# A two-layer backbone: R and KK as halves of one tile, joint grams, and another order around the recurrence

## Chip, cores and metric

One core of one Trainium2 chip runs the whole program. The metric is device time in microseconds, the median of the runs shown. Engines: TensorE (PE; its weight loads are listed apart as PEld), VectorE (DVE), ScalarE (ACT), GpSimd (POOL), and SyncE (SP), which issues most DMAs.

## The reference, cut to what matters

Two layers work on 768 tokens (256 context, 512 latent) of 1024 channels. In each layer one projection feeds three branches (a bidirectional RWKV-7 recurrence, a convolution of width 31, attention), which are merged; an MLP follows. The change is in the recurrence. For each head of 64 channels and each direction, a state S of 64 x 64 runs over the tokens:

```python
def step(S, inp):
    r_t, w_t, k_t, v_t, kk_t, a_t = inp
    s_kk = jnp.einsum('bhij,bhj->bhi', S, kk_t)
    S = (S * w_t[:, :, None, :]
         - s_kk[..., None] * (kk_t * a_t)[:, :, None, :]
         + v_t[..., None] * k_t[:, :, None, :])
    return S, jnp.einsum('bhij,bhj->bhi', S, r_t)
```

Before it, kk is normalised per head and decays come from a small two-step projection; after it, a "readout" normalises y per head, adds a bonus (a sum over r, keys and r_k, times v) and multiplies by a gate. In layer 1 the context needs no output: there r and the readout are computed for the 512 latent tokens only (T = 512; `lat` is true).

## The kernel before, in words

Channels lie on partitions, two heads (a "pair", rows 0 to 63 and 64 to 127) per 128 partitions; 8 pairs per layer. The 768 tokens are 12 chunks of 64. In chunked form the recurrence of a pair consists of:

- `rw_kk`, `rw_decay`, `rw_keys`, `rw_rows`, `rw_rrows`: elementwise work on VectorE and ScalarE that makes, per direction d, the tile BK (per chunk the two kinds of keys divided by the decay, 128 columns), KK (kk times the decay, `in_k` and `in_kk` reused) and R (r times the decay, `sg` and `in_r` reused). L803 makes KK, L819 makes R. `rw_bonus` starts with L910, which must read r before L819 overwrites it.
- the grams: `rw_lgram` (L830) multiplies BK of a chunk with KK of the chunk, `rw_rgram` (L847) BK with R; each product has 64 columns. VectorE masks the results into GL (L832) and GB (L850). `rw_rgram` also transposes BK (L857) into GB's other half and copies R into KR (L852).
- `rw_seed` and `rw_solve`: the triangular solve on VectorE (L899, L900), in tile A; `rw_rest`: KK transposed and GL times V (L883), on TensorE.
- in the weave of the next pair: `rw_merge`, `rw_batch` (L963, L974), then `rw_chain`, 12 steps in order of time. A step carries the state (L995, L999, scaled by ScalarE at L1001) and adds to the output y the part from the state (L1011) and the part that needs no state (L1013). `rw_readout` ends the pair one weave later.

All this is small work. The large one, the 128-column jobs of the input projection (`fill`, L412; weights split by L328 on ScalarE and L332 on VectorE), is laid between it. `weave` goes round a list of generators, and each `yield us` calls `pe(us)`, which issues `us * ratio` jobs, and `taps`, which issues taps of the convolution on VectorE (L472). While pair p runs merge, batch, chain, pair p+1 goes from kk to solve in the same weave; `wait` and `note` tie the generators together (`b0`, `b1`: batch of a direction done; `s3`, `s7`, `s11`: chain steps done). The ratio of a weave is the number of jobs over `span`, 84 in both layers. The tile framework's own planner may still exchange neighbouring instructions of an engine's queue by its costs.

PSUM tiles for the small work come from `s.g`, two buffers; a gram takes both, one per head. Tiles named by `rt` share memory by alias: `a1` holds ksq, the spread sums, the decay of direction 0 (`sg`) and, for the readout, ysq and the bonus read back; `a2` and `a3` are the halves of A.

Of the kernel before, what the change touches and what calls it, by code (L numbers as in the profile page):

```python
# [21 lines left out]
CTX = 256  # L22
# [25 lines left out]
SCHED = [dict(open=1.3, early=4, tap0=1, tap2=0, step=1.0, merge=1.2, sums=0, rest=9, ln=9, pad=1, last=1.15, span=84),  # L48
         dict(open=1.2, early=5, tap0=0.8, tap2=0, step=1.0, merge=1.4, sums=0, rest=9, ln=9, pad=1, last=0.85, span=84)]
# [27 lines left out]
class Kern:  # L77
# [580 lines left out]
    def rt(s, tag, shape, bufs=1, alias=None):  # L658
        n = int(np.prod(shape[1:]))
        if alias in s.parts:  # L660
            return s.A[:, s.parts[alias]:s.parts[alias] + n]
# [53 lines left out]
    def rw_kk(s, P, p, I):  # L715
# [3 lines left out]
        sq = s.rt("ksq", [128, TOK], alias="a1")  # L719
# [8 lines left out]
        rn = s.head_spread(rn, 0, "a1")  # L728
# [66 lines left out]
    def rw_rows(s, I, Q, lat):  # L795

        nc = s.nc
        k, kk, o = I['k'], I['kk'], CTX if lat else 0
# [5 lines left out]
        Q['KK'] = (k, kk)  # L804
        yield 0.4
# [5 lines left out]

    def rw_rrows(s, I, Q, lat):

        nc, o = s.nc, CTX if lat else 0
        while 'r' not in I or 'bonus' not in Q:
            yield 0.1
# [3 lines left out]
        Q['R'] = (Q['sg', 0], r)  # L820
        yield 0.3

    def rw_lgram(s, Q, d, c0, n):

        nc = s.nc
        BK, GL, KK = s.big['BK', d], s.big['GL', d], s.c64(Q['KK'][d])
        gp = [s.g([128, n, 64]) for h in range(2)]
        for q in range(n):
            for h in range(2):
                nc.tensor.matmul(gp[h][:, q, :], lhsT=BK[ROWS[h], c0 + q].rearrange("p a b -> p (a b)"), rhs=KK[ROWS[h], c0 + q, :], start=True, stop=True)  # L830
        for h in range(2):
            nc.vector.tensor_tensor(out=GL[:, h, c0:c0 + n], in0=gp[h], in1=s.mask(d, h, 0).unsqueeze(1).to_broadcast([128, n, 64]), op=ALU.mult)  # L832
        yield 0.2 * n

    def rw_rgram(s, Q, part, lat):

        nc = s.nc
        cs = [slice(4 * a, 4 * a + 4) for a in ((0, 0), (1, 2), (2, 1))[part]]
        BK, GB, KR = ([s.big[x, d] for d in range(2)] for x in ('BK', 'GB', 'KR'))
        if part or not lat:  # L840
            R = [s.c64(x) for x in Q['R']]
            gp = [s.g([128, 2, 4, 64]) for h in range(2)]
            for d in range(2):
                for q in range(4):
                    u = cs[d].start + q
                    for h in range(2):
                        nc.tensor.matmul(gp[h][:, d, q, :], lhsT=BK[d][ROWS[h], u].rearrange("p a b -> p (a b)"), rhs=R[d][ROWS[h], u, :], start=True, stop=True)  # L847
            for d in range(2):
                for h in range(2):
                    nc.vector.tensor_tensor(out=GB[d][:, h, cs[d], 1], in0=gp[h][:, d], in1=s.mask(d, h, 1).unsqueeze(1).to_broadcast([128, 4, 64]), op=ALU.mult)  # L850
            for d in range(2):
                nc.scalar.activation(out=KR[d][:, 1, cs[d]], in_=R[d][:, cs[d]], func=AF.Copy)  # L852
            yield 1.4
        for d in range(2):
            bk = s.g([128, 4, 2, 64])
            for q in range(4):
                nc.tensor.transpose(out=bk[:, q].rearrange("p a b -> p (a b)"), in_=BK[d][:, cs[d].start + q].rearrange("p a b -> p (a b)"), identity=s.ident)  # L857
            nc.scalar.activation(out=GB[d][:, :, cs[d], 0, :], in_=bk.rearrange("p c h j -> p h c j"), func=AF.Copy)
            yield 0.45
# [14 lines left out]
    def rw_rest(s, Q, d):  # L874
# [11 lines left out]
        for h in range(2):  # L886
            s.rw_transpose(Q['KK'][d], h, lambda par: KM[ROWS[h], par::2, 0, :])
# [92 lines left out]
    def rw_chain(s, Q, lat, note, free):  # L980
# [5 lines left out]
        for k in range(NCH):  # L986
# [15 lines left out]
            if need_y:  # L1002
                fresh = seg not in yp
                if fresh:
                    yp[seg] = s.py.tile([128, 512], F32, tag="y", name="yp")
                for part in ((1, 0) if k else (0,)):
                    for d in range(2):
                        o = (q[d] - 4 * seg) * 64
                        for h in range(2):
                            if part:  # L1010
                                nc.tensor.matmul(yp[seg][ROWS[h], o:o + 64], lhsT=KR[d][ROWS[h], 1, q[d], :], rhs=S[ROWS[h], d], start=fresh, stop=False)  # L1011
                            else:
                                nc.tensor.matmul(yp[seg][ROWS[h], o:o + 64], lhsT=GB[d][:, h, q[d], 1, :], rhs=UV[d][:, h * 12 + q[d], :], start=fresh, stop=d == 1 and k in (3, NCH - 1))  # L1013
                        fresh = False
# [10 lines left out]
    def rw_readout(s, l, P, p, Q, T, dst):  # L1025
# [9 lines left out]
        sq = t("ysq", [128, TOK], alias="a1")  # L1035
# [3 lines left out]
        bv = t("bv", [128, TOK], alias="a1")  # L1039
# [134 lines left out]
    def rwkv_phase(s, l, P, T):  # L1174
# [3 lines left out]
        with ExitStack() as rc:  # L1178
            s.rp = rc.enter_context(tc.tile_pool(name="rw", bufs=1))
            s.alias, s.parts = {'a1': 768}, {'a2': 0, 'a3': 768}  # L1180

            s.A = s.rp.tile([128, 1536], F32, name="A")
            s.dw = s.conv_taps(l, s.rp)
# [26 lines left out]
            def prep(p, I, Q, wait, *held):  # L1210
# [5 lines left out]
            def sums(p, I, Q, wait, note):  # L1216

                return chain(wait('keys'), s.after(I, 'r', 0, chain(par(s.rw_bonus(P, p, I, Q, T), chain(s.rw_rrows(I, Q, lat), note('rows'))))))
# [11 lines left out]
            def grams(I, Q, wait):  # L1230

                return chain(wait('s3', 'rows'), s.rw_rgram(Q, 0, lat), wait('s7'), s.rw_rgram(Q, 1, lat), wait('s11'), s.rw_rgram(Q, 2, lat),
                             s.rw_values(I), s.rw_rest(Q, 0), s.rw_rest(Q, 1))
# [18 lines left out]
            def stages(p, I, Q, wait, note, *held):  # L1252
                g = prep(p, I, Q, wait, *held)
                return [chain(keyed(g, I, Q, note), solve()), sums(p, I, Q, wait, note), grams(I, Q, wait)]

            def keyed(g, I, Q, note):

                done = False
                for us in g:
                    if not done and 'KK' in Q:  # L1260
                        done = True
                        yield from note('keys')
                    yield us
# [6 lines left out]
            ev, wait, note = events('b0', 'b1', 's3', 's7', 's11')  # L1270
            s.weave(F['open'], *stages(0, I, Q, wait, note))
            old = None
            for p in range(8):
                ev, wait, note = events()
                more = p < 7
                if more:
# [3 lines left out]
                    s.conv_jobs(l, P, p + 1, T, s.ocv)  # L1280
# [227 lines left out]
```

## Time and profile before

| | |
|---|---|
| median of 3 runs | 4574.11 us (4558.41 to 4584.1) |
| profiled execution | 4581.7 us |
| its span, first to last instruction | 4579.9 us |
| instructions | 79160 |
| mean granted TensorE clock | 0.938 |
| TensorE / VectorE / ScalarE busy | 95% / 59% / 40% of the span |
| recurrence of layer 0, about | 60 to 1460 us |
| recurrence of layer 1, about | 2640 to 3820 us |

The span is that of the profiled execution alone; 1.8 us of its own time lie around it. A matmul is recorded with the time until its result has drained, and its neighbours overlap it: what one costs is read from start to start, and a group's "busy" is the union of its instructions. The granted clock is a share of full speed, so 0.5 is the lower of two levels.

### The profile page before, as it was taken

The numbers are of one execution on the slowest core, as the hardware profiler recorded it, in microseconds if no ns is written. First come the engines' busy times: TensorE is split into PE (matmuls) and PEld (weight loads), VectorE is DVE, ScalarE is ACT, GpSimd is POOL, SyncE is SP. The second block draws the span as 40 slices with busy tenths as digits, with TensorE's granted clock in tenths as the row PEclk, the third lists the DMA queues.
The fourth block names the chain that finished last, engine by engine and source line by source line (L and its number), as shares of the span: only waits on it lengthen the run. The fifth ranks groups of instructions, "written<-read, shape, count | busy, mean of one in ns | idle before, by whom it ended". The sixth has DMA issues, their size and how long they took to land. (4 is left out here: it accounts for less than half of the span.)

```text
span 4579.9 us, 79160 instructions
## 1 busy us (share of the span) xinstructions
PE 4346.8 (95%) x32512; PEld 3601.1 (79%) x32512; DVE 2719.8 (59%) x5062; ACT 1838.2 (40%) x3474; POOL 255.3 (6%) x221
## 2 busy tenths in 40 slices
PE   6999999999999989899999899999999999898998
PEld 4988888888887669689999677877777785575886
DVE  3677778877873555342333567777786765464344
ACT  3344444444443443332222444444453434444333
POOL 0000000000001021200000100000000001031001
PEclk9899899999999999999999888999897979999998
DMA  4211111111134225443322221111121124142332
GB/s 164 68 41 51 54 57 50 54 48 63 49 97 149 80 91 161 136 138 113 106 88 63 72 59 50 55 56 44 51 61 49 57 70 139 46 139 72 95 96 79
DMA packets 443601, 367.87 MB, mean 80 GB/s; under 512 B 19662, under 2 KB 391528, under 8 KB 437096
## 3 DMA queue, kind: packets, MB, share of 16 engines
q1 hardware_dynamic: 422504, 283.10, 20.6%
q10 hardware_dynamic: 20736, 79.70, 4.8%
q8 instruction: 257, 4.21, 0.4%
q14 instruction: 104, 0.85, 0.1%
HBM read 301.38 MB, written 53.48 MB: 77 GB/s over the span
## 5 line engine op out<-in xcount | busy, mean ns | idle before, releaser
L332 DVE TENSOR_TENSOR wl<-raw,wh 128x512 fp32r<-128x512 f32 x700 | 504.4, 721 | 743.6 <-ACT wh L328 718.2
L328 ACT ACTIVATE wh<-raw 128x512 fp32r<-128x512 f32 x700 | 441.4, 631 | 1210.8 <-PE mm L412 565.3
L412 PE MATMUL mm<-hh,wh 128*128 128x384 f32 (+1 forms) x2072 | 671.4, 384 | 13.2 <-ACT hh L347 4.0
L412 PE MATMUL mm<-hl,wh 128*128 128x384 f32 (+1 forms) x2072 | 646.0, 371 | 6.1 <-POOL hl L330 6.1
L412 PE MATMUL mm<-hh,wl 128*128 128x384 f32 (+1 forms) x2072 | 648.8, 372 | 0.9 <-DVE wl L332 0.9
L412 PEld LDWEIGHTS mm<-hh,wh 128*128 128x128 f32 x2072 | 377.8, 196 | 66.0 <-issue 11.3
L472 DVE SCALAR_TENSOR_TENSOR cv<-u,dw,cv 128x783 f32<-128x783 f32 (+1 forms) x480 | 426.6, 889 | 3.9
L412 PEld LDWEIGHTS mm<-hl,wh 128*128 128x128 f32 x2072 | 391.8, 195 | 38.2 <-POOL hl L330 8.8
L412 PEld LDWEIGHTS mm<-hh,wl 128*128 128x128 f32 x2072 | 393.5, 196 | 32.2 <-issue 4.4
L412 PE MATMUL mm<-oh,wh 128*128 128x384 f32 (+1 forms) x768 | 253.1, 384 | 10.2 <-DVE acc L1334 5.5
L412 PE MATMUL mm<-ol,wh 128*128 128x384 f32 (+1 forms) x768 | 241.4, 367 | 8.6 <-POOL ol L330 8.6
L389 PE MATMUL mm<-hh,wh 128*128 128x384 f32 (+1 forms) x768 | 238.0, 365 | 6.4 <-ACT hh L347 3.6
L389 PE MATMUL mm<-hl,wh 128*128 128x384 f32 (+1 forms) x768 | 237.1, 363 | 6.4 <-POOL hl L330 5.9
L412 PE MATMUL mm<-oh,wl 128*128 128x384 f32 (+1 forms) x768 | 239.3, 365 | 0.0
L389 PE MATMUL mm<-hh,wl 128*128 128x384 f32 (+1 forms) x768 | 234.8, 360 | 0.0
L389 PE MATMUL mm<-fh,wh 128*128 128x384 f32 (+1 forms) x768 | 230.0, 353 | 0.0
L389 PE MATMUL mm<-fh,wl 128*128 128x384 f32 (+1 forms) x768 | 229.9, 353 | 0.0
L389 PE MATMUL mm<-fl,wh 128*128 128x384 f32 (+1 forms) x768 | 229.4, 352 | 0.0
L1001 ACT ACTIVATE S<-sp,lam 128x64 f32<-128x64 f32 x352 | 92.1, 310 | 226.6 <-PE sp L999 210.4
L412 PEld LDWEIGHTS mm<-oh,wh 128*128 128x128 f32 x768 | 140.2, 190 | 51.6 <-ACT wh L328 13.6
L389 PEld LDWEIGHTS mm<-hh,wh 128*128 128x128 f32 x768 | 141.5, 191 | 37.7 <-ACT wh L328 15.9
L900 DVE TENSOR_TENSOR A<-A,Z 128x30 f32<-128x30 f32 (+14 forms) x480 | 158.9, 331 | 12.9
(311 smaller groups left out, 7566.4 us busy)
## 6 DMA issues: line engine op xcount, KB each, us to landing
raw<-in_w_in_dram SPq DMA_DIRECT2D x316, 256.0 KB
raw<-in_w_ff_dram SPq DMA_DIRECT2D x256, 256.0 KB
wmod<-in_w_mod_dram ACTq DMA_DIRECT2D x48, 1024.0 KB
raw<-in_w_branch_dram SPq DMA_DIRECT2D x96, 256.0 KB
z<-f ACTq DMA_DIRECT2D x40, 384.0 KB
gt<-z SPq DMA_DIRECT2D x24, 384.0 KB
raw<-in_w_out_dram SPq DMA_DIRECT2D x32, 256.0 KB
z<-f ACTq DMA_DIRECT2D x32, 256.0 KB
```

The lines of the kernel that those rows point to most:

```text
L328: s.last_hi = nc.scalar.activation(out=hi, in_=src, func=AF.Copy)
L332: nc.vector.tensor_tensor(out=lo, in0=src, in1=hi.bitcast(F32), op=ALU.subtract)
L389: nc.tensor.matmul(ps[:, b, :t1 - t0], lhsT=w[:, k % 4, :], rhs=a[:, t0:t1], start=k == 0 and f == 0, stop=k == KT - 1 and f == 2)
L412: s.last_mm = nc.tensor.matmul(s.jps[:, b, :t1 - t0], lhsT=w[:, k % 4, :], rhs=a[:, t0:t1], start=k == 0 and f == 0, stop=k == KT - 1 and ...
L472: s.tap_pin(nc.vector.scalar_tensor_tensor(out=hold['c'], in0=u[:, k:k + L], scalar=w(k), in1=hold['c'], op0=ALU.mult, op1=ALU.add))
L900: nc.vector.tensor_tensor(out=X[:, k + 1:, 0:k], in0=X[:, k + 1:, 0:k], in1=tm, op=ALU.add)
L1001: nc.scalar.activation(out=Sn[:, d], in_=sp[:, d], func=AF.Copy, scale=Q['lam', d][:, q[d]:q[d] + 1])
```

## The change

Per direction d there is a new tile `E[d]` of 2 x 768 columns: KK in its first half, R in its second. `in_k`, the decay of direction 0, `in_kk` and `in_r` are now parts of the two tiles, so nothing is copied to get there. `rw_front` multiplies BK of a chunk with both halves at once (128 columns; in layer 1's first four chunks with KK alone), four chunks per call, and masks both results. `rw_turn` (transposes of BK) and `rw_readers` (R into KR, one copy per direction) are what is left of `rw_rgram`. R is made inside `rw_rows`, so before the first gram. The decay's last exponentials move ahead of a yield. In `rw_chain`, all stateless products of a segment (4 or 8 chunks) are issued at the segment's first step, then `y0` or `y1` is noted; the fronts of the next pair wait for `y1`, since they write GB. kk, the readout of the pair before and the decays advance side by side (`par`) instead of one after the other. Before the weave of a pair, 8 to 15 jobs are issued at once; `span` is 78 and 76. The readout's squares and bonus now live in `key`, kk's squares and spread sums in `a2`.

```diff
-SCHED = [dict(open=1.3, ..., last=1.15, span=84),
-         dict(open=1.2, ..., last=0.85, span=84)]
+SCHED = [dict(open=1.3, ..., last=1.15, span=78),
+         dict(open=1.2, ..., last=0.85, span=76)]
...
-        sq = s.rt("ksq", [128, TOK], alias="a1")
+        sq = s.rt("ksq", [128, TOK], alias="a2")
...
-        rn = s.head_spread(rn, 0, "a1")
+        rn = s.head_spread(rn, 0, "a2")
...
     def rw_rows(s, I, Q, lat):
...
-        Q['KK'] = (k, kk)
-        yield 0.4
         for d in range(2):
             Q['lam', d] = s.rt("lam%d" % d, [128, 12], 2)
             e = Q['sg', d]
             nc.scalar.activation(out=e, in_=e, func=AF.Exp, scale=CDEC)
             nc.gpsimd.tensor_copy(Q['lam', d], s.c64(e)[:, :, 63 * (1 - d)])
-
-    def rw_rrows(s, I, Q, lat):
-
-        nc, o = s.nc, CTX if lat else 0
-        while 'r' not in I or 'bonus' not in Q:
+        yield 0.4
+        while 'bonus' not in Q:
             yield 0.1
         r = I['r']
         for d, to in ((0, Q['sg', 0]), (1, r)):
             nc.vector.tensor_tensor(out=to[:, o:], in0=r[:, o:], in1=Q['sg', d][:, o:], op=ALU.mult)
-        Q['R'] = (Q['sg', 0], r)
-        yield 0.3
+        yield 0.2
+
+    def rw_front(s, d, g, lat):
+
+        nc = s.nc
+        c = slice(4 * g, 4 * g + 4)
+        n = 1 if lat and g == 0 else 2
+        BK, GL, GB = (s.big[x, d] for x in ('BK', 'GL', 'GB'))
+        E = s.E[d].rearrange("p (x c t) -> p x c t", x=2, t=64)
+        gp = [s.g([128, 4, 2, 64]) for h in range(2)]
+        for q in range(4):
             for h in range(2):
-                nc.tensor.matmul(gp[h][:, q, :], lhsT=BK[ROWS[h], c0 + q].rearrange("p a b -> p (a b)"), rhs=KK[ROWS[h], c0 + q, :], start=True, stop=True)
...
+                nc.tensor.matmul(gp[h][:, q, 0:n, :], lhsT=BK[ROWS[h], 4 * g + q].rearrange("p a b -> p (a b)"),
+                                 rhs=E[ROWS[h], 0:n, 4 * g + q, :], start=True, stop=True)
+        for x, G in ((0, GL[:, :, c]), (1, GB[:, :, c, 1]))[:n]:
+            for h in range(2):
+                nc.vector.tensor_tensor(out=G[:, h], in0=gp[h][:, :, x, :],
+                                        in1=s.mask(d, h, x).unsqueeze(1).to_broadcast([128, 4, 64]), op=ALU.mult)
+        yield 1.0
...
+    def rw_readers(s, lat):
+
+        o = 4 if lat else 0
         for d in range(2):
+            s.nc.scalar.activation(out=s.big['KR', d][:, 1, o:], in_=s.c64(s.E[d][:, TOK:])[:, o:], func=AF.Copy)
+        yield 0.2
...
             if need_y:
-                fresh = seg not in yp
-                if fresh:
+                off = lambda c: (c - 4 * seg) * 64
+                if seg not in yp:
                     yp[seg] = s.py.tile([128, 512], F32, tag="y", name="yp")
-                for part in ((1, 0) if k else (0,)):
+                    for c in (range(4, NCH) if seg else range(4)):
+                        for d in range(2):
+                            for h in range(2):
+                                nc.tensor.matmul(yp[seg][ROWS[h], off(c):off(c) + 64], lhsT=GB[d][:, h, c, 1, :], rhs=UV[d][:, h * 12 + c, :], start=c == 4 * seg and d == 0, stop=False)
+                    note("y%d" % seg)
+                if k:
...
-        sq = t("ysq", [128, TOK], alias="a1")
+        sq = t("ysq", [128, TOK], alias="key")
...
-        bv = t("bv", [128, TOK], alias="a1")
+        bv = t("bv", [128, TOK], alias="key")
...
-            s.alias, s.parts = {'a1': 768}, {'a2': 0, 'a3': 768}
+
+            s.E = [s.rp.tile([128, 2 * TOK], F32, name=f"E{d}") for d in range(2)]
...
+            s.key = s.rp.tile([128, TOK], F32, name="key")
+            s.alias, s.parts = {}, {'in_k': (s.E[0], 0), 'a1': (s.E[0], TOK), 'in_kk': (s.E[1], 0), 'in_r': (s.E[1], TOK),
+                                    'a2': (s.A, 0), 'a3': (s.A, 768), 'key': (s.key, 0)}
...
-                return chain(s.after(I, 'k', 0, s.rw_kk(P, p, I)), *held, s.rw_decay(P, p, Q), wait('b0'), s.rw_keys(P, p, I, Q, 0), wait('b1'), s.rw_keys(P, p, I, Q, 1),
-                             s.rw_rows(I, Q, lat), *(s.rw_lgram(Q, d, c, n) for d in (1, 0) for c, n in ((0, 8), (8, 4))), wait('rows'),
+                return chain(par(s.after(I, 'k', 0, s.rw_kk(P, p, I)), chain(*held), s.rw_decay(P, p, Q)),
+                             wait('b0'), s.rw_keys(P, p, I, Q, 0), wait('b1'), s.rw_keys(P, p, I, Q, 1), note('keys'),
+                             s.rw_rows(I, Q, lat), wait('y1'), *(s.rw_front(d, g, lat) for d in (1, 0) for g in (1, 2, 0)),
                              s.rw_seed(1, slice(0, 12)), s.rw_seed(0, slice(0, 12)))
...
+                return chain(wait('keys', 's3'), s.rw_turn(0, 0), s.rw_turn(1, 0), wait('s7'), s.rw_turn(0, 1), s.rw_turn(1, 2), wait('s11', 'rows'), s.rw_turn(0, 2), s.rw_turn(1, 1),
+                             s.rw_readers(lat), s.rw_values(I), s.rw_rest(0), s.rw_rest(1))
...
                     s.conv_jobs(l, P, p + 1, T, s.ocv)
+                    s.fill(8 + len(s.jobs) % 8)
```

## Rows read from the trace of the kernel before

**Rows 1.** The page, busy us, share of the span and instructions per engine.

```profile
PE 4346.8 (95%) x32512; PEld 3601.1 (79%) x32512; DVE 2719.8 (59%) x5062; ACT 1838.2 (40%) x3474; POOL 255.3 (6%) x221
```

**Rows 2.** Windows, both recurrences: length, busy us (instructions) per engine, granted clock, DMA.

```profile
60.00:1460.00 1400.00, 1371.40 (x13029) 1197.83 (x13030) 1021.16 (x1915) 604.31 (x1209) 22.37 (x40) 0.94 0.20 62
2640.00:3820.00 1180.00, 1130.07 (x10565) 911.22 (x10564) 847.24 (x1730) 533.97 (x1092) 13.11 (x34) 0.89 0.20 60
```

**Rows 3.** Groups by line on PE: out<-in, shapes, count | busy us, mean ns.

```profile
L830 PE MATMUL g<-in_k,BK 64*128 64x64 f32 x768 | 121.2, 348 | 0.0
...
L847 PE MATMUL g<-sg,BK 64*128 64x64 f32 x640 | 95.0, 332 | 0.0
...
L847 PE MATMUL g<-in_r,BK 64*128 64x64 f32 x640 | 88.2, 329 | 0.0
...
L830 PE MATMUL g<-in_kk,BK 64*128 64x64 f32 x768 | 83.0, 323 | 32.4 <-DVE in_kk L803 31.3 <-DVE GL L832 1.1
...
L1013 PE MATMUL yp<-UV,GB 128*64 128x64 f32 x1280 | 76.5, 237 | 0.0
```

**Rows 4.** Timeline of PE, grams of layer 0: start us, us, instruction, count.

```profile
637.90 2.00 PE L830 MATMUL g<-in_kk,BK 64*128 64x64 f32 x32
639.84 0.44 PE L412 MATMUL mm<-hl,wh 128*128 128x384 f32 x1
...
641.08 1.10 PE L830 MATMUL g<-in_kk,BK 64*128 64x64 f32 x8
642.11 0.44 PE L412 MATMUL mm<-hl,wh 128*128 128x384 f32 x1
```

**Rows 5.** Timeline of PE, runs with 64-column weights, layer 0.

```profile
683.64 1.02 PE L883 MATMUL g<-UV,GL 64*64 64x64 f32 x26
684.59 0.44 PE L412 MATMUL mm<-hh,wl 128*128 128x384 f32 x1
...
716.04 1.96 PE L963 MATMUL g<-BK,GL 64*64 64x128 f32 x32
717.94 0.61 PE L412 MATMUL mm<-hh,wh 128*128 128x384 f32 x2
```

**Rows 6.** Windows of 2 us around the grams of that pair, layer 0.

```profile
646.00:648.00 2.00, 2.00 (x26) 2.00 (x25) 1.63 (x4) 0.00 (x0) 0.00 (x0) 1.00 0.00 0
...
656.00:658.00 2.00, 2.00 (x14) 1.88 (x14) 0.94 (x3) 0.00 (x0) 0.00 (x0) 0.50 0.00 0
...
674.00:676.00 2.00, 2.00 (x19) 1.75 (x17) 1.79 (x7) 0.46 (x1) 0.00 (x0) 1.00 0.74 237
```

**Rows 7.** Timeline of PE, first grams of a pair of layer 1.

```profile
3081.91 3.68 PE L830 MATMUL g<-in_kk,BK 64*128 64x64 f32 x32 [7.30 <-DVE in_kk L803]
3085.52 0.79 PE L412 MATMUL mm<-hh,wl 128*128 128x512 f32 x1
```

**Rows 8.** Waits of PE, layer 0, then layer 1: us, times, longest.

```profile
PE g L830 <- DVE in_kk L803: 2.2, 1, 2.2
...
PE g L830 <- DVE in_kk L803: 29.1, 7, 7.3
```

**Rows 9.** Timeline of DVE ahead of that wait, idle time in brackets.

```profile
3055.03 0.75 DVE L1056 SCALAR_TENSOR_TENSOR y<-y,V,bv 128x512 f32<-128x512 f32 x1 [3.12 <-ACT y L1054]
...
3061.13 1.76 DVE L765 TENSOR_TENSOR_SCAN sg<-smask,sg 128x768 f32<-128x768 uint8 x1 [4.09 <-ACT sg L763]
...
3080.90 0.95 DVE L803 TENSOR_TENSOR in_kk<-in_kk,Z 128x768 f32<-128x768 f32 x1
...
3082.98 0.68 DVE L819 TENSOR_TENSOR in_r<-in_r,A 128x512 f32<-128x512 f32 x1
```

**Rows 10.** Groups by line and shape on DVE: the masks.

```profile
L832 DVE TENSOR_TENSOR GL<-g,masks 128x512 f32<-128x512 f32 x64 | 42.5, 688 | 48.6 <-PE g L830 48.4
L832 DVE TENSOR_TENSOR GL<-g,masks 128x256 f32<-128x256 f32 x64 | 26.9, 424 | 79.1 <-PE g L830 78.6
```

**Rows 11.** Window of 20 us behind the wait of layer 1's pair.

```profile
3098.00:3118.00 20.00, 20.00 (x100) 17.59 (x99) 8.25 (x20) 6.33 (x11) 0.00 (x0) 0.57 0.16 48
```

More of the change, by code (lines that the diff above doesn't have):

```diff
@@ L44 @@
 VOFF = {n: 8 * i for i, n in enumerate(VECS)}
-SCHED = [dict(open=1.3, early=4, tap0=1, tap2=0, step=1.0, merge=1.2, sums=0, rest=9, ln=9, pad=1, last=1.15, span=84),
-         dict(open=1.2, early=5, tap0=0.8, tap2=0, step=1.0, merge=1.4, sums=0, rest=9, ln=9, pad=1, last=0.85, span=84)]
+SCHED = [dict(open=1.3, early=4, tap0=1, tap2=0, step=1.0, merge=1.2, sums=0, rest=9, ln=9, pad=1, last=1.15, span=78),
+         dict(open=1.2, early=5, tap0=0.8, tap2=0, step=1.0, merge=1.4, sums=0, rest=9, ln=9, pad=1, last=0.85, span=76)]
 def shape_constants():
@@ L835, in rw_rgram @@
[L835 to L853, printed above, removed]
-        for d in range(2):
[L855 to L859, printed above, removed]
@@ new lines, in rw_front, with rw_turn @@
+        for x, G in ((0, GL[:, :, c]), (1, GB[:, :, c, 1]))[:n]:
[3 more added lines that the diff above has]
+        yield 1.0
+    def rw_turn(s, d, g):
+        nc, c = s.nc, slice(4 * g, 4 * g + 4)
+        BK, GB = (s.big[x, d] for x in ('BK', 'GB'))
+        bk = s.g([128, 4, 2, 64])
+        for q in range(4):
+            nc.tensor.transpose(out=bk[:, q].rearrange("p a b -> p (a b)"), in_=BK[:, 4 * g + q].rearrange("p a b -> p (a b)"), identity=s.ident)
+        nc.scalar.activation(out=GB[:, :, c, 0, :], in_=bk.rearrange("p c h j -> p h c j"), func=AF.Copy)
+        yield 0.45
@@ L1002, in rw_chain @@
             if need_y:
[L1003 to L1004 removed]
+                off = lambda c: (c - 4 * seg) * 64
+                if seg not in yp:
                     yp[seg] = s.py.tile([128, 512], F32, tag="y", name="yp")
[L1006 removed]
+                    for c in (range(4, NCH) if seg else range(4)):
[4 more added lines that the diff above has]
+                if k:
                     for d in range(2):
[L1008 removed]
                         for h in range(2):
[L1010 to L1014, printed above, removed]
+                            nc.tensor.matmul(yp[seg][ROWS[h], off(q[d]):off(q[d]) + 64], lhsT=KR[d][ROWS[h], 1, q[d], :], rhs=S[ROWS[h], d], start=False, stop=d == 1 and k in (3, NCH - 1))
             S = Sn
@@ L1209, in chain, with prep @@
                     yield from g
-            def prep(p, I, Q, wait, *held):
-                return chain(s.after(I, 'k', 0, s.rw_kk(P, p, I)), *held, s.rw_decay(P, p, Q), wait('b0'), s.rw_keys(P, p, I, Q, 0), wait('b1'), s.rw_keys(P, p, I, Q, 1),
-                             s.rw_rows(I, Q, lat), *(s.rw_lgram(Q, d, c, n) for d in (1, 0) for c, n in ((0, 8), (8, 4))), wait('rows'),
+            def prep(p, I, Q, wait, note, *held):
+                return chain(par(s.after(I, 'k', 0, s.rw_kk(P, p, I)), chain(*held), s.rw_decay(P, p, Q)),
+                             wait('b0'), s.rw_keys(P, p, I, Q, 0), wait('b1'), s.rw_keys(P, p, I, Q, 1), note('keys'),
+                             s.rw_rows(I, Q, lat), wait('y1'), *(s.rw_front(d, g, lat) for d in (1, 0) for g in (1, 2, 0)),
                              s.rw_seed(1, slice(0, 12)), s.rw_seed(0, slice(0, 12)))
-            def sums(p, I, Q, wait, note):
-                return chain(wait('keys'), s.after(I, 'r', 0, chain(par(s.rw_bonus(P, p, I, Q, T), chain(s.rw_rrows(I, Q, lat), note('rows'))))))
             def par(*gs):
@@ L1228, in par, with rests @@
                             yield us
-            def grams(I, Q, wait):
-                return chain(wait('s3', 'rows'), s.rw_rgram(Q, 0, lat), wait('s7'), s.rw_rgram(Q, 1, lat), wait('s11'), s.rw_rgram(Q, 2, lat),
-                             s.rw_values(I), s.rw_rest(Q, 0), s.rw_rest(Q, 1))
+            def rests(I, wait):
+                return chain(wait('keys', 's3'), s.rw_turn(0, 0), s.rw_turn(1, 0), wait('s7'), s.rw_turn(0, 1), s.rw_turn(1, 2), wait('s11', 'rows'), s.rw_turn(0, 2), s.rw_turn(1, 1),
+                             s.rw_readers(lat), s.rw_values(I), s.rw_rest(0), s.rw_rest(1))
             def events(*ns):
@@ L1252, in stages @@
             def stages(p, I, Q, wait, note, *held):
[L1253 to L1263, printed above, removed]
+                return [chain(prep(p, I, Q, wait, note, *held), note('rows'), solve()),
+                        chain(wait('keys'), s.after(I, 'r', 0, s.rw_bonus(P, p, I, Q, T))), rests(I, wait)]
             todo_c = lambda p: round((32 - F['rest']) * p / 7)
```

22 lines of the change are left out of this document (8 added, 14 removed).

## The prediction, made before the result was known

> **What bounds the kernel now.** I read the busy shares first: TensorE is busy for 95% of the span, VectorE for 59%, ScalarE for 40% [rows 1]. Then the windows of the two stretches that the change touches, the recurrence of layer 0 and of layer 1: TensorE is busy 1371 of 1400 us and 1130 of 1180 us, VectorE 1021 and 847 us [rows 2]. So TensorE's instruction stream sets the time there, with 28.6 and 49.9 us of gaps; VectorE has about a quarter to spare on average. The same rows give a mean granted clock of 0.94 and 0.89. With two levels, full and half, that is half clock (1.2 GHz) for 12% of 1400 and 22% of 1180, 168 + 260 = 428 us, and costs half of it, 214 us.
>
> Next the costliest instructions of the part that changes. The grams are L830 (with KK) and L847 (with R): 121.2 + 83.0 + 95.0 + 88.2 = 387 us busy for 2 x 768 + 2 x 640 = 2816 instructions, 137 ns each [rows 3]. The code asks for 24 products per direction and pair, 384 in 16 pairs, where the trace counts 768: each fp32 product is two instructions. All are 64 columns against 128-column weights on half of the rows.
>
> The order in time gives their price at full clock, start to start: 32 in 1.94 us, 61 ns each, where the two heads (the two halves of the rows) alternate; 8 in 1.03 us, 129 ns, in a run that I read as one head's, since four chunks give eight instructions per head [rows 4]. In layer 1 the same 32 take 3.61 us after a gap of 7.30 us [rows 7], 113 ns each, at half clock. The clock also falls without a gap: at 646 it is 1.00, at 656 it is 0.50 with TensorE recorded busy for the whole 2 us, at 674 it is back [rows 6]. What ran there was almost only grams.
>
> Last, who is waited for: the first gram waits for VectorE's `in_kk` (L803) once in layer 0 (2.2 us) and 7 times in layer 1, 29.1 us [rows 8]. Before that wait VectorE itself stood still for 3.12 and 4.09 us, behind the readout's copies (L1054) and then behind the decay's ScalarE step (L763) [rows 9]: readout and decay run one after the other.
>
> **The change, part by part.**
>
> (a) Both grams of a chunk in one product of 128 columns. 1280 R instructions and as many of KK become 1280; the 256 of KK left over (layer 1's first four chunks, which need no output: 1536 - 1280) stay. What the 64 further columns cost isn't in the trace for these weights. Nearest rows: with 64-column weights, 26 instructions of 64 columns take 0.95 us (37 ns) and 32 of 128 columns 1.90 us (59 ns), so 64 columns more cost 23 ns where halves alternate [rows 5]; in a one-head run nothing alternates and I take twice that, 46. So a chunk's pair goes from 2 x 61 = 122 to 61 + 23 = 84 ns, and from 258 to 129 + 46 = 175: 31 to 32% less; I use 30. The pairs cost now 183 us (L847) plus 1280/1536 of L830's 204, 170 us: 353 us. 0.30 x 353 = **106 us gained**. Bounds: 0, if the columns alone set the price, and 177 (half of 353), if the weights alone do. I take 106, because both kinds of row show a part that goes with the weights and one that goes with the columns.
>
> (b) Readout, kk and decays side by side, and 8 to 15 jobs issued ahead of each pair's weave, so that k is there when it begins. VectorE's two gaps, 7.2 us together, are as long as the wait of 7.30 us that follows [rows 7, 9]; filling them removes it. Of the 31.3 us of these waits [rows 8] I take **20 gained**; bounds 0 and 31. The jobs ahead are moved, not added: TensorE runs them anyway.
>
> (c) The first gram now needs R too, so it waits for r's product (L819) and not for `in_kk`. In the pair shown `in_kk` begins at 3080.90 and is done 0.95 later, r's product begins at 3082.98 and takes 0.68: 1.8 us later [rows 9]. Queued behind it on TensorE is everything, ordinary jobs included. What covers it is the projection work that the order puts there; without cover 16 x 1.8 = 29 us. I take **15 lost**; bounds 0 and 29.
>
> (d) Stateless outputs of a segment together. The same 1280 instructions, now in runs of 32 and 64 instead of eights; 76.5 us busy, 60 ns each [rows 3]. The long run of 64 columns in [rows 5] went at 37 ns at full clock, so at most (60 - 37) x 1280 = 29 us, and at least nothing, since a part of the 60 is half clock; I stay near the lower end, since the runs that grow are no shorter in columns. **5 gained**.
>
> (e) Masks on VectorE: in a pair of layer 0, 4 of 512 elements and 16 of 256 become 24 of 256: 4 x 0.69 + 16 x 0.42 = 9.5 us against 10.1 [rows 10], 0.6 us more per pair. It hides in VectorE's spare quarter; if not, 10 us in all. Six copies of R on ScalarE become two large ones, on an engine 40% busy: nothing. The squares and spread sums move into the solve's tile A, so they wait for the solve's last transposes; the merge at the same place waits for those already, so nothing. No DMA is added; the bonus reload and g2 are issued earlier on SP's queue, ahead of weights that have slack: nothing.
>
> (f) Clock. Fewer gram instructions in a row, with jobs between, and no gap ahead of them: some of the 214 us comes back. The gram's own part is in (a) already; the jobs that run inside the half-clock stretches are not. **20 gained**, about a tenth; bounds 0 and 107, half.
>
> Sum: 106 + 20 - 15 + 5 + 20 = **136 us gained**. The profiled execution took 4581.7 us; that gives 4446. The median of the runs shown is 4574.1, 7.6 lower, so a median should come out at 4438: I predict **4440**, 3% less.
>
> **Rivals.**
>
> *Weights alone set a gram's price.* Then (a) is 177: 4581.7 - 207 - 7.6 = 4367, and with half of the clock back 4280. For it: 61 ns against 37 for the same columns with half the weights [rows 4, 5]. Against: 23 ns more for the columns in the same rows. Chance 0.2.
>
> *Nothing saved in the grams.* If loads are hidden behind the other head's columns, two products of 64 columns equal one of 128. (a) is 0, and the rest leaves 30 us: 4544; with the waits as they are, 4574. For it: L830 is recorded as busy without a break. Against: the 61 to 37 ns above. Chance 0.11. The Trainium skill, "TensorE: Matmul & The Clock Gate", section "Part 2: What happens when you issue a matmul", speaks for this rival: it says the engine pulls a weight load ahead of running matmuls when their row groups don't conflict, which is just the case of two heads. By that rule the sum would be 30 us instead of 136. This trace agrees only in part: alternating heads do cost 61 ns instead of 129, but the width of the weights still shows.
>
> *Slower: the gate before the first gram.* Now three VectorE products more than before stand between keys and grams in one chain (L803, then the bonus's, then L819). If the order puts no jobs there, every pair stands still as layer 1's do, 7.3 us, and half clock follows: I price that at the 7.3 us and at 0.43 x 20 = 8.6 us lost to the clock in a window of 20 us behind such a wait, granted 0.57 [rows 11]: 16 us per pair, 16 x 16 = 256, against the 151 us of the other terms: 4574 + 105 = 4679. It decides from 151/16 = 9.4 us per pair. For it: seven of layer 1's eight pairs wait there now [rows 8]. Against: layer 0 waits once only, and (b) fills the gaps from which the wait comes. Chance 0.09.
>
> **The numbers.** My forecast has 0.6; its own range is 4390 to 4510, from (a) at 60 to 150 us. Over all cases the range is 4350 to 4560: it takes in the weights-alone case and the nothing-saved case, and leaves out the slower one and the best of the clock. About 0.5% (23 us) is what a measurement of this kernel can tell from no change. Faster by more than that: 0.6 + 0.2 + 0.03 = 0.83; within: 0.08; slower: 0.09.
>
> **What would show it.** Gram instructions: 1536 instead of 2816, with about 85 ns each where heads alternate and busy time near 280 us in place of 387. The wait of the first gram on VectorE, now for r's product, under 31 us in all. Mean granted clock in the recurrences at or above 0.94 and 0.89. Windows of both recurrences about 8 us per pair shorter, TensorE still over 96% busy. I'm wrong if grams keep 115 ns or more per instruction at full clock, or if TensorE's gaps in the recurrences grow by over 60 us.

## The result and the profile after

The changed kernel takes 4303.18 us (median; 4295.91 to 4305.05) against 4574.11 us of the kernel before: ratio 0.9409, 95% interval 0.9373 to 0.9444, so 271 us or 5.9% less. A fourth run of the kernel before took 5619.48 us, far from its other three, and is left out of both figures. The result is faster, as predicted, but 137 us below the forecast of 4440 and 47 us below the range. The profiled execution took 4305.05 us, with a span of 4303.3 us.

The page after, busy us and share of the span per engine, answers to [rows 1]:

```profile
PE 4083.1 (95%) x31232; PEld 3360.6 (78%) x31232; DVE 2712.4 (63%) x5126; ACT 1829.2 (43%) x3426; POOL 254.8 (6%) x221
```

TensorE is busy 263.7 us less with 1280 instructions fewer, and its gaps (span less busy) go from 233.1 to 220.2 us. The two make the 276.6 us by which the span is shorter. VectorE and ScalarE have as much to do as before.

The windows of the recurrences after (length, busy us per engine, granted clock) answer to [rows 2]; layer 1 now begins earlier:

```profile
60.00:1460.00 1400.00, 1366.53 (x12805) 1165.87 (x12806) 1090.74 (x2088) 665.24 (x1312) 39.47 (x49) 0.98 0.23 72
2480.00:3680.00 1200.00, 1146.11 (x10657) 887.49 (x10656) 929.63 (x1943) 604.85 (x1223) 23.75 (x42) 0.96 0.23 71
```

TensorE is the bound as before; its granted clock rose from 0.94 and 0.89 to 0.98 and 0.96, and over the whole span from 0.938 to 0.969. With two levels that is 2 x (1 - 0.938) x 4579.9 = 568 us at half clock before and 267 us after: 301 us less, worth 150 us. After, the recurrences end some 170 us before these windows do, before some 40. From a layer's first product into y to its last, it took 1152 us before and 1032 after in layer 0, and 1016 and 897 in layer 1: 119 us less in each, 15 us per pair.

The gram and stateless groups after (busy us, mean ns | idle before, its releasers) answer to [rows 3]; L828 is the joint gram, L1001 the stateless output:

```profile
L828 PE MATMUL g<-E,BK 64*128 64x128 f32 x1280 | 125.7, 285 | 12.6 <-ACT key L912 6.9 <-DVE GB L832 3.3 <-DVE E L815 2.1
L1001 PE MATMUL yp<-UV,GB 128*64 128x64 f32 x1280 | 54.9, 226 | 0.0
L828 PE MATMUL g<-E,BK 64*128 64x64 f32 x256 | 20.3, 277 | 0.3 <-DVE GB L832 0.2
```

The four groups of [rows 3] can't simply be added up for a comparison: the two with R (95.0 and 88.2 us) run in between each other and overlap. Busy time of their line, L847, in the kernel before, with the overlap counted once (length, PE, its loads, clock, DMA):

```profile
0.00:4580.00 4580.00, 150.46 (x1280) 143.68 (x1280) 0.94 0.26 80
```

With L830's 204.15 us, and 2 us in which the two lines overlap, grams cost 352.5 us before for 2816 instructions, 125 ns each, and not the 387 us that the prediction went by. After, they cost 146.0 us for 1536, 95 ns each. So 206 us went: 1280 x 125 = 160 by the count, and 1536 x (125 - 95) = 46 because each of the others is cheaper too. What made those cheaper is the clock. By the starts and the granted clock in the two traces, 1096 of the 2816 instructions began at half clock, on average 176 ns ahead of the next start, and the other 1720 took 88 ns; after, none of the 1536 began at half clock, and they took 90 ns. At full clock, 1280 instructions fewer are worth 1280 x 88 = 113 us. With 150 us of clock and 13 us of gaps that makes the 276 us of the span.

The lines also show the waits ahead of the grams: 12.9 us in all, 2.1 of them on r's product (L815), where [rows 8] had 31.3 us.

Around them, the jobs of the projection (L412 with `hh` and `hl`), 6216 instructions before and after, fell from 1962.5 to 1903.3 us; the transposes from 70.6 to 56.8; the stateless outputs from 76.5 to 54.9. (Groups overlap at their edges and the rest grew by 13 us, so these sum to more than 263.7.)

TensorE's timeline after, layer 0 (start us, us, instruction, count), gives the price start to start, as [rows 4] did:

```profile
300.91 1.16 PE L828 MATMUL g<-E,BK 64*128 64x128 f32 x16
302.00 0.33 PE L1006 MATMUL yp<-S,KR 64*64 64x64 f32 x2
...
310.68 1.16 PE L828 MATMUL g<-E,BK 64*128 64x128 f32 x8
311.76 0.44 PE L412 MATMUL mm<-hh,wh 128*128 128x384 f32 x1
```

16 joint instructions in 1.09 us, 68 ns each; 8 in 1.08 us, 135 ns each. With half of the columns it was 61 (in a run of 32) and 129. I had put 23 and 46 ns on the 64 further columns; they cost 7 and 6 at most, and nothing between runs of one length (split and double, below).

### The profile page after: what moved, and what is told of

It reads as the page before. It is cut to its first block, busy times and chain, and to the rows that moved or that the text cites. A ratio compares the mean times of both kernels' runs of the same rounds, so it can differ in the third digit from the quotient of the medians.

```text
span 4303.3 us, 76623 instructions
## 1 busy us (share of the span) xinstructions
PE 4083.1 (95%) x31232; PEld 3360.6 (78%) x31232; DVE 2712.4 (63%) x5126; ACT 1829.2 (43%) x3426; POOL 254.8 (6%) x221
## 4 chain that ended last, share of the span: by engine, by line
PE 78%; DVE 11%; ACT 4%; issue 3%; DMA 2%; POOL 2%; SPq 0%; ACTq 0%; DVEq 0%; POOLq 0%
PE mm L412 29%; PE mm L389 21%; PE g L828 3%; PE g L634 2%; PE g L955 2%; PE g L966 2%; PE sp L987 2%; PE sp L991 2%; PE S L613 1%; PE g L875 1%; PE g L1071 1%; PE yp L1006 1%; DVE wl L332 1%; DVE A L892 1%; DVE Z L891 1%
## 5 line engine op out<-in xcount | busy, mean ns | idle before, releaser
L412 PE MATMUL mm<-hh,wh 128*128 128x384 f32 (+1 forms) x2072 | 658.9, 378 | 10.0 <-ACT hh L347 4.0
L412 PE MATMUL mm<-hl,wh 128*128 128x384 f32 (+1 forms) x2072 | 626.0, 362 | 7.2 <-POOL hl L330 7.2
L412 PE MATMUL mm<-hh,wl 128*128 128x384 f32 (+1 forms) x2072 | 619.1, 361 | 2.5 <-DVE wl L332 2.4
L412 PEld LDWEIGHTS mm<-hh,wh 128*128 128x128 f32 x2072 | 367.8, 191 | 61.8 <-issue 9.8
L412 PEld LDWEIGHTS mm<-hl,wh 128*128 128x128 f32 x2072 | 383.9, 191 | 34.4 <-POOL hl L330 10.0
L412 PEld LDWEIGHTS mm<-hh,wl 128*128 128x128 f32 x2072 | 384.0, 192 | 29.8 <-DVE wl L332 4.5
L412 PE MATMUL mm<-oh,wh 128*128 128x384 f32 (+1 forms) x768 | 252.3, 383 | 10.4 <-DVE acc L1320 6.0
L412 PE MATMUL mm<-ol,wh 128*128 128x384 f32 (+1 forms) x768 | 240.0, 365 | 10.6 <-POOL ol L330 10.6
L389 PE MATMUL mm<-hh,wh 128*128 128x384 f32 (+1 forms) x768 | 239.1, 366 | 6.3 <-ACT hh L347 3.6
L389 PE MATMUL mm<-hl,wh 128*128 128x384 f32 (+1 forms) x768 | 238.2, 365 | 5.5 <-POOL hl L330 5.0
L412 PE MATMUL mm<-oh,wl 128*128 128x384 f32 (+1 forms) x768 | 239.4, 365 | 0.0
L389 PE MATMUL mm<-hh,wl 128*128 128x384 f32 (+1 forms) x768 | 235.8, 362 | 0.0
L412 PEld LDWEIGHTS mm<-oh,wh 128*128 128x128 f32 x768 | 139.9, 190 | 51.5 <-ACT wh L328 13.6
L389 PEld LDWEIGHTS mm<-hh,wh 128*128 128x128 f32 x768 | 142.2, 192 | 37.7 <-ACT wh L328 15.9
```

Source lines behind the costliest of these rows:

```text
L389: nc.tensor.matmul(ps[:, b, :t1 - t0], lhsT=w[:, k % 4, :], rhs=a[:, t0:t1], start=k == 0 and f == 0, stop=k == KT - 1 and f == 2)
L412: s.last_mm = nc.tensor.matmul(s.jps[:, b, :t1 - t0], lhsT=w[:, k % 4, :], rhs=a[:, t0:t1], start=k == 0 and f == 0, stop=k == KT - 1 and ...
```

## The experiments

Two theories. **Count and price:** a gram costs its weight load, so half as many loads is the gain. **Runs of one half:** where the planner lets one half of the rows stand alone for eight instructions, each costs twice as much and the clock falls with them; the change gains because it has fewer of these. The rival to both is the order of the work around the grams. All runs, with grams as instructions x columns, their mean busy ns each (overlaps counted once), and the mean granted clock of the span:

| run | grams | ns | clock | us, median | ratio to before |
|---|---|---|---|---|---|
| before | 2816 x 64 | 125 | 0.938 | 4572 to 4577 | 1 |
| changed kernel | 1280 x 128, 256 x 64 | 95 | 0.969 | 4303.18 | 0.9409 [0.9373, 0.9444] |
| split | 2816 x 64 | 101 | 0.951 | 4473.95 | 0.9779 [0.9744, 0.9813] |
| double | 2560 x 128, 512 x 64 | 77 | 0.964 | 4421.13 | 0.9681 [0.9637, 0.9725] |
| onehead | as changed | 119 | 0.967 | 4323.21 | 0.9463 [0.9409, 0.9517] |
| serial | as changed | 106 | 0.967 | 4328.98 | 0.9461 [0.9425, 0.9498] |
| noprefill | as changed | 101 | 0.970 | 4325.59 | 0.9454 [0.9421, 0.9487] |
| joint_old_order | as changed | 107 | 0.965 | 4348.11 | 0.9520 [0.9477, 0.9564] |
| split_old_order | 2816 x 64 | 107 | 0.944 | 4490.33 | 0.9827 [0.9765, 0.9889] |
| before_y | as before | 123 | 0.942 | 4567.35 | 1.0007 [0.9978, 1.0037] |
| before_late | as before | 130 | 0.930 | 4606.25 | 1.0078 [1.0041, 1.0115] |
| before_pin | as before | 84 | 0.964 | 4438.99 | 0.9713 [0.9669, 0.9757] |
| before_late_pin | as before | 81 | 0.962 | 4469.98 | 0.9766 [0.9715, 0.9818] |
| pinned | as changed | 93 | 0.966 | 4352.39 | 0.9514 [0.9480, 0.9549] |
| split_pin | 2816 x 64 | 78 | 0.966 | 4428.31 | 0.9678 [0.9619, 0.9738] |
| before_four | as before | 105 | 0.949 | 4545.05 | 0.9936 [0.9911, 0.9961] |
| before_late_four | as before | 135 | 0.922 | 4694.7 | 1.0237 [1.0157, 1.0316] |

**split, double: loads or columns.** Both start from the changed kernel. split issues each joint product as two of 64 columns; double issues it twice at 128.

```diff
+            for x in range(n):                                          # split
                 for h in range(2):
-                    nc.tensor.matmul(gp[h][:, q, 0:n, :], ... rhs=E[ROWS[h], 0:n, 4 * g + q, :], ...)
+                    nc.tensor.matmul(gp[h][:, q, x, :], ... rhs=E[ROWS[h], x, 4 * g + q, :], ...)
+            for twice in range(2):                                      # double: the loop over h, twice
```

> The changed kernel, but each joint product of 128 columns issued again as two products of 64 columns with the same weights: 2816 gram instructions instead of 1536, all else (order, jobs ahead, stateless outputs together) as changed. Theory A, the joint products did it, by their number and through the clock: the gain over the kernel before mostly goes, 4303 + about 87 (1280 more at 68 ns) + most of the clock's part, so 4450 to 4580, with the granted clock of the recurrences back near 0.95 and 0.90. Theory B, the new order gave the clock back and the joint products only saved instructions: 4303 + 80 to 100 = about 4390, granted clock still 0.98 or more.

> The changed kernel with every joint product issued twice (the second overwrites the first with the same values), so 3072 gram instructions of 128 columns: as many weight loads as with split products (2816), with twice the columns. If the number of weight loads sets both price and clock: 4303 + 171 x 1536/1280 = about 4508, half clock around the grams as with split products. If the columns per load decide about the clock: 4303 + 1536 x 68 to 75 ns = 4410 to 4420, granted clock as in the changed kernel (0.98 and 0.96).

The timeline of split, then that of double, for one run of 32 each:

```profile
324.23 2.06 PE L829 MATMUL g<-E,BK 64*128 64x64 f32 x32
326.22 0.63 PE L412 MATMUL mm<-hh,wl 128*128 128x384 f32 x2
```

```profile
302.21 2.06 PE L829 MATMUL g<-E,BK 64*128 64x128 f32 x32
304.19 0.33 PE L1007 MATMUL yp<-S,KR 64*64 64x64 f32 x2
```

32 of 64 columns in 1.99 us and 32 of 128 columns in 1.98: 62 ns each, so in these runs the further columns cost nothing. By that price the 1280 instructions of split are worth 79 us, but split lost 171. The rest goes with the clock: 0.951 is 438 us at half clock, against 267 in the changed kernel, and half of the difference is 86 us; 79 + 86 = 165. In double, with about as many loads (3072 against 2816) and twice the columns, the clock is 0.964, 318 us at half: 1536 x 62 = 95 us and 26 of clock make 121, and it lost 118. The jobs show the clock too: 1940.1 us in split against 1904.8 in double and 1903.3 in the changed kernel.

**onehead: the halves one after the other.** The changed kernel with the two loops exchanged.

```diff
-        for q in range(4):
-            for h in range(2):
+        for h in range(2):
+            for q in range(4):
```

> The changed kernel with the joint products of a call in the other order: four chunks of one head, then four of the other. From the timeline, 68 ns per instruction where heads alternate and 136 where one head runs alone. If that is so, the grams' 146 us busy go to about 1536 x 136 = 209, and the time to 4303 + 60 = 4365, or a little more if the clock falls. If the order of heads doesn't matter: 4303 within 10 us.

```profile
L828 PE MATMUL g<-E,BK 64*128 64x128 f32 x1280 | 150.7, 289 | 6.7 <-DVE E L815 2.2 <-ACT key L912 2.1 <-ACT KR L850 1.2
L828 PE MATMUL g<-E,BK 64*128 64x64 f32 x256 | 34.5, 293 | 0.0
```

These gram groups are 183.0 us together (overlaps counted once), 37 more than before the exchange, and the time grew by 20, not by the 60 expected: many of the changed kernel's groups ran one half alone already (the eights in its timeline). As I read it, the planner exchanges neighbours by when the two PSUM tiles come free; no run shows that. The clock stayed at 0.967 (0.969 in the changed kernel), though more of the joint grams ran as one half alone.

**serial, noprefill, joint_old_order, split_old_order: the order.** serial puts kk, readout and decay one after the other again; noprefill drops the jobs issued ahead; joint_old_order does both and sets `span` to 84, split_old_order adds split.

```diff
-                return chain(par(s.after(I, 'k', 0, s.rw_kk(P, p, I)), chain(*held), s.rw_decay(P, p, Q)),
+                return chain(s.after(I, 'k', 0, s.rw_kk(P, p, I)), *held, s.rw_decay(P, p, Q),
...
-                    s.fill(8 + len(s.jobs) % 8)
```

> The changed kernel with kk, the readout and the decays one after the other again; joint products kept. Theory A (joint products): 4303 to 4330, clock as in the changed kernel. Theory B (the order gave the clock back): 4380 or more, granted clock in layer 1's recurrence under 0.95, waits of the first gram on VectorE back at about 30 us.

> The changed kernel without the 8 to 15 jobs issued ahead of each pair's weave. Theory A: 4303 to 4330. Theory B: 4350 or more, with the first products of the merge waiting for the solve (now 7.7 us in all) and lower granted clock at the start of the pairs.

> The changed kernel with the joint products kept, and the order taken back: kk, readout and decays one after the other, no jobs issued ahead of the weave, span 84 again. If the small effects of these (25 and 22 us, each alone) simply add, 4350; a theory in which one of them covers for the other says 4400 or more, and waits of the first gram on VectorE of 20 us or more as in the kernel before.

> As the kernel joint_old_order, with each joint product split in two products of 64 columns. What stays of the change is the grouping (grams of KK and R of four chunks together, after R is made) and the stateless outputs. Theory A, the splitting costs the same whatever the order: joint_old_order + 171, about 4520. Theory B, the grouping is worth nothing and the rest of the distance was order: within 15 us of the kernel before, 4560 to 4585.

serial loses 26 us, noprefill 22, both together 45: they add. In joint_old_order TensorE is busy for 4085.7 us, as with the new order (4083.1), but its span is 4349.6, so its gaps are 263.9 us and not 220.2. The order's gain is 44 us of gaps. Most of it is one wait of joint_old_order (us, times, longest):

```profile
PE g L909 <- DVE key L902: 40.7, 8, 9.8
```

L909 is TensorE's product in `rw_bonus`, which waits for VectorE's first product there; in the changed kernel it waits 1.7 us. Joint products are worth 4490 - 4348 = 142 us in the old order and 171 in the new one.

**before_y: the stateless outputs alone.** The kernel before with the change's loop over a segment's stateless products in place of its own, and nothing else.

> The kernel before with one part of the change alone: the stateless outputs of a segment issued together at its first step. Both theories: a small gain, 5 to 30 us, 4545 to 4570, from 76.5 us busy for these products down to 50 to 70; half clock around the grams as in the kernel before.

```profile
L1009 PE MATMUL yp<-UV,GB 128*64 128x64 f32 x1280 | 48.0, 229 | 0.0
```

These products take 48.0 us in place of 76.5, and the time is the same. Where those 28 us went isn't shown: the profile is of an execution of 4553.33 us, 14 less than the median.

**before_late, before_four, before_late_four: 87 us not accounted for.** split_old_order has the gram instructions of the kernel before and takes 87 us less. Two parts of the difference were tried on the kernel before, alone and together: the gate ahead of the KK grams, and groups of four chunks. The edit shown is both.

```diff
-                             s.rw_rows(I, Q, lat), *(s.rw_lgram(Q, d, c, n) for d in (1, 0) for c, n in ((0, 8), (8, 4))), wait('rows'),
+                             s.rw_rows(I, Q, lat), wait('rows'), *(s.rw_lgram(Q, d, c, n) for d in (1, 0) for c, n in ((0, 4), (4, 4), (8, 4))),
```

> The kernel before with its KK grams issued only after R is made (as the change does it, but separate products of 64 columns in the old groups). If the distance between the kernel before (4577) and split_old_order (4490) comes from the first gram, which no longer waits for VectorE (31 us) and no longer drops the clock behind such a wait: 4510 to 4545, wait on L803 under 5 us. If it comes from how the two heads follow each other in the grams: within 15 us of 4577.

> The kernel before with the KK grams in three groups of four chunks per direction in place of eight and four; nothing else. Theory A (groups of four release their two PSUM tiles sooner and are what split_old_order has over the kernel before): 40 to 87 us faster, 4490 to 4535, fewer gram us (under 370 of 387 before). Theory B (smaller groups only give the planner more places to put one half alone): no change or slower, 4575 to 4600, gram busy time at 387 us or more.

> The kernel before with both: KK grams in groups of four, and the wait for the readout's rows ahead of them (before_late alone: 4606). Theory A: well under before_late, 4510 to 4560. Theory B: at or above before_late, 4600 or more; then the 87 us of split_old_order come from KK and R of a chunk standing next to each other, and not from the size of a group or the place of the gate.

The later gate alone costs 32 us. The wait on L803 is gone, but TensorE now waits 37.5 us for the bonus's product instead (L917 on L910), and the clock fell to 0.930. Groups of four alone gain 27 us. Both times lie outside of both ranges expected.

```profile
L830 PE MATMUL g<-in_kk,BK 64*128 64x64 f32 x768 | 93.5, 339 | 62.3 <-DVE in_kk L803 62.2
```

There the waits of the first gram doubled, from 31.3 to 62.2 us, and yet the kernel is faster, since the grams fell from 352.5 to 295.1 us. Both together lose 123 us. TensorE's gaps grew from 233.1 to 283.0 us there, and its longest wait is again for the bonus:

```profile
PE g L917 <- DVE key L910: 73.7, 9, 14.2
```

The clock fell too, to 0.922. A window of before_late_four (length, busy us per engine, granted clock):

```profile
816.00:862.00 46.00, 46.00 (x217) 41.40 (x217) 17.87 (x42) 6.54 (x11) 0.00 (x0) 0.52 0.09 26
```

TensorE is recorded busy for all of 46 us, with no gap, at a clock of 0.52. So neither gate nor group size by itself accounts for the 87 us. The grams hold 52 us of it (352.5 before, 300.6 in split_old_order), but before_four's 295.1 are no dearer, and it is still 55 us slower than split_old_order. It waits more: 62.2 us for L803, where split_old_order waits 33.4 us for the bonus. What is left (among other things KK and R of a chunk next to each other, the transposes apart from the grams, two copies of R in place of six) wasn't isolated.

**before_pin, before_late_pin, pinned, split_pin: the order of the halves.** `tap_pin` is the kernel's own helper that keeps an instruction in the order in which the code writes it. Put around the gram products alone, it makes the halves alternate.

```diff
-                nc.tensor.matmul(gp[h][:, q, :], lhsT=BK[...]..., rhs=KK[ROWS[h], c0 + q, :], start=True, stop=True)
+                s.tap_pin(nc.tensor.matmul(gp[h][:, q, :], lhsT=BK[...]..., rhs=KK[ROWS[h], c0 + q, :], start=True, stop=True))
```

> The kernel before with the gram instructions kept in the order of the program on TensorE, so that the two heads alternate throughout (61 ns instead of 129 where one head ran alone). If the one-head runs made the grams dear: gram busy from 387 to under 320 us, time 4577 - 60 to 90 = 4490 to 4520. If the wait of the first gram is the cause: within 15 us of 4577.

> Both of these edits. If the two causes share the 87 us to split_old_order, this kernel comes to 4490 within 20 us; if the grouping by four chunks with R counts by itself, it stays above 4520.

> The changed kernel with its joint products kept in the order of the program, so that heads alternate throughout: 62 to 68 ns instead of 136 where one head ran alone. The grams' 146 us busy go to about 1536 x 68 = 104; if TensorE's stream sets the time, 4303 - 30 to 42 = 4261 to 4273. Rival: a product that must not be overtaken makes the others wait for the masks of the call before (two PSUM tiles only), and the time stays within 10 us of 4303 or rises.

> The changed kernel with each joint product as two products of 64 columns, and these written into TensorE's order so that the two row halves alternate. Compare with pinned (4352, the same with joint products) and split (4474, no pin). Theory (alternating runs cost 62 ns per instruction whatever the columns, and keep the clock): 1280 further instructions at 62 ns are 79 us over pinned, about 4430, half-clock time in both recurrences near 160 to 200 us where split has 331. Rival (64-column products lower the clock as such, alternating or not): half-clock time stays near 330 us and the time near 4470 or above.

The kernel before, with this and nothing else, is 136 us faster. Its groups, against [rows 3]:

```profile
L830 PE MATMUL g<-in_kk,BK 64*128 64x64 f32 x768 | 74.2, 334 | 34.8 <-DVE in_kk L803 34.0 <-DVE GL L832 0.8
L830 PE MATMUL g<-in_k,BK 64*128 64x64 f32 x768 | 64.4, 280 | 0.0
L847 PE MATMUL g<-sg,BK 64*128 64x64 f32 x640 | 61.4, 281 | 0.1
L847 PE MATMUL g<-in_r,BK 64*128 64x64 f32 x640 | 50.8, 272 | 0.0
```

With overlaps counted once that is 235.7 us for the same 2816 instructions (352.5), with the wait on L803 still there at 34.0 us. Where its grams run and where those of the kernel before ran, first before_pin, then the kernel before (timeline, layer 0):

```profile
608.70 1.10 PE L830 MATMUL g<-in_kk,BK 64*128 64x64 f32 x14
609.73 0.61 PE L412 MATMUL mm<-hh,wh 128*128 128x384 f32 x2
```

```profile
658.97 1.97 PE L830 MATMUL g<-in_k,BK 64*128 64x64 f32 x8
660.87 1.11 PE L857 MATMUL g<-cst,BK 128*128 128x128 f32 x4
```

14 in 1.03 us, 74 ns each, and no eights; before, 8 in 1.90 us, 238 ns each: one half alone, and at half clock. Of the 1096 gram instructions that began at half clock, 305 are left.

before_late_pin shows the gate where halves alternate: 31 us slower than before_pin, with 55.7 us of waits for the bonus where before_pin waits 34.0 us on L803.

The pinned pair is the cleanest measure of the count. pinned and split_pin differ in 1280 gram instructions, and both have a clock of 0.966: 4428.31 - 4352.39 = 76 us, 59 ns per instruction, where 79 us were expected. The rival, that products of 64 columns lower the clock as such, falls: split_pin has them. Both theories hold, then: the count is worth 76 us where the halves alternate, and the alternation 136 us where the count stays.

Pinning the changed kernel costs 49 us. Its grams as a whole fell by 3 us only (143.3), as the first two instructions of many groups run by themselves and the other 14 later. TensorE's busy time grew by 25 us and its gaps by 23; which order it gave up for that stays open. No run beats the changed kernel.

## Why the prediction was wrong

Its direction and its place were right: the bound stayed TensorE's stream, and most of the gain came out of the grams. But the case that came nearest is the rival *weights alone* (4367, or 4280 with half of the clock back), which had 0.2, and not the forecast. The runs split the gain in three: 87 us from the kernel before to split_old_order, 142 from there to joint_old_order (the joint products), 45 to the changed kernel (the order). The prediction had 106 for the products, 20 for the order, and for all the rest, (c), (d) and (f), 10 together. So two terms were mis-sized most, (a) and (f).

**(a), the price of 64 further columns: the step that failed.** I took 23 ns from [rows 5] and added it to the 61 ns of the load. Measured: 62 ns at 64 and at 128 columns. The four alternating prices at hand are 37 ns (64-column weights, 64 columns), 59 (64, 128), 62 (128, 64) and 62 (128, 128): the larger of the two sets it, they don't add. So a pair of products costs half, not 30% less. The base was wrong the other way: 387 us counted the overlap of two groups twice, and the pairs cost 150 + 170 = 320 us, not 353. Half of that is 160 us, and the grams gave 206, because the instructions that stay also left half clock. The joint products alone, all else kept, are worth 142 to 171 us.

The Trainium skill, "TensorE: Matmul & The Clock Gate", "Part 2: What happens when you issue a matmul", was behind the rival *nothing saved*: loads are pulled ahead when row groups differ. Here alternating halves do cost half of what one half alone does (62 against 129), so loads overlap something; but they aren't hidden under the columns, since split and double cost the same per load. The same part, under "Back-to-back issue gap", gives some 62 ns per matmul for the sequencer when it decodes in microcode, and the 62 ns of the runs of 32 fit; but inside these runs the starts lie 56 ns apart on average, and the 37 ns of [rows 5] are below it too, so the load and not the sequencer is the likelier cause here.

**(f), the clock: 20 us, bound 107; the other step that failed.** The span's half-clock time fell by 301 us, worth 150. The grams themselves spent 1096 x 176 = 193 us at half clock, so 96 of the 150 are in their price above; outside them the jobs alone, with the same instructions, are 59 us cheaper. I had seen in [rows 6] that the clock falls without a gap, read that almost only grams ran there (of the 28 us from 646 to 674 they took 15.3, jobs 9.0), and priced it as an accident. It goes with the eights that I read as one half's runs in [rows 4]. before_pin makes the halves alternate and changes nothing else in the code, and the clock goes from 0.938 to 0.964.

**(b), the order: 20 predicted, 45 measured**, as gaps: 263.9 to 220.2 us. The bound of 31 counted the wait on L803; the new gate moves it to the bonus's product, 40.7 us in joint_old_order, and that is the wait which the order fills.

**(c), the later gate: 15 lost predicted.** In the changed kernel the waits ahead of the grams are 12.9 us in all, and the bonus's 1.7. Without the new order the same gate costs 32 us in the kernel before, by a longer wait at another place and by the clock. The rival *slower* has this much truth: in before_late_four nine waits for the bonus make 73.7 us, and 123 us are lost.

**(d), the stateless outputs: 5 predicted, none measured. (e):** right; VectorE and ScalarE are busy 7 and 9 us less.

Of the signs named, 1536 instructions, the clock and the waits came as said; the grams' busy time (146, not 280), the price of alternating runs (68, not 85 ns) and the time per pair (15 us less, not 8) showed the steps that were off. TensorE is busy 97.6% of layer 0's window and 95.5% of layer 1's, a little under the 96%.

**Still open:** which part of the change holds the 87 us between the kernel before and split_old_order, and what pinning costs the changed kernel.

## What to carry to other kernels

When two small products share their weights, join them: price the joint one at the larger of weight columns and moving columns, not at their sum, and price the saved ones at the clock and the alternation that the trace shows. Where small products use half of the rows, look at the order in which the halves reach the engine: runs of one half cost twice as much each and can take the clock of everything around them, and keeping the written order was worth 136 us in the kernel before with no other edit, though it cost 49 us in the changed one. A wait that vanishes is no gain by itself: before_late lost the wait on L803 and got a longer one for the bonus, and before_four was faster with twice the wait. And add up busy times of groups only where they don't interleave: 387 us of grams were 352.5.

## What the runs showed of the hardware

- fp32 products with 128-column weights on half of the rows: 62 ns per instruction at 64 and at 128 columns where the halves alternate (runs of 32, split and double); 129 and 135 in runs of eight, one half alone. Between the starts inside such runs lie 112 ns for two instructions that alternate and 112 ns for each one of a half alone.
- The granted clock was near its lower level with TensorE recorded busy without a gap: 0.52 over 46 us in before_late_four. Grams, transposes and jobs ran there. Recorded busy time doesn't tell whether the clock holds.
- The clock of the span was 0.951 with products of 64 columns (split) and 0.964 with as many of 128 (double); with the halves kept alternating it was 0.966 at 64 (split_pin) and at 128 (pinned).
